# A two-layer decoder trunk: the first two weight tiles in halves, and the last 256 tokens as twice 128

## The chip, the cores and the metric

The kernel runs on one core of a Trainium2 chip. The metric is the time of one execution on the device in microseconds (us), lower is better. Three runs of the kernel before took 2276.80, 2274.09 and 2271.59 us; their median, 2274.09 us, is the time before.

## What is computed

The reference is a decoder trunk of two layers over 1024 tokens with a model width of 1024, in float32. Cut to what matters here:

```python
for l in range(2):
    h = rms_norm(x, norm1[l])
    z = h @ w_in[l]                       # pool | gate u, v | q, k, v
    mix = concat(pool_mixer(...), spatial_gate(...), stick_breaking_attention(q, k, v))
    x = x + mix @ w_out[l]
    h = rms_norm(x, norm2[l])
    x = x + relu(h @ w_up[l])**2 @ w_down[l]   # inner width 4096
return rms_norm(x, final_norm)
```

## The kernel before

**Layout.** Activations lie transposed: 128 features on the partitions, tokens along the free dimension, so x is 8 feature tiles k by 2 chunks c of 512 tokens (chunk 1 holds the first half, as tokens run in reverse). Every matrix product takes its operands as a rounded part and the rest ("hi" and "lo"): `split` (L155 on ScalarE, L156 on VectorE) makes the two, and `mm3` (L235 to L250) adds three products per tile: hi by hi (L243), lo by hi (L248 or L249, by which operand is meant) and hi by lo. A weight tile is 128 rows by 1024 columns; `load_w` fetches it by one DMA of 512 KB into `raw` (L231) and splits it into `wh` and `wl`.

**What sets the order.** The Python code states the work; a tile scheduler then orders the instructions of each engine by its own model of their times, with raised priority for some (`early(W_EARLY)` for the splits of weights, `early(EVAC_EARLY)` for adds that free a PSUM bank). Each engine runs its own list in order. A change of one early instruction can therefore move instructions elsewhere in the lists.

**The start of layer 0.** `load_x` (L477) fetches x tile by tile, all on SyncE's queue: x tile 0, the first weight tile (key columns of the first head pair), x tiles 1 to 3, the second weight tile (query columns), x tiles 4 to 7, then the other chunk. `use_x` scales each x tile by the norm's gain and splits it (`put_x`: ScalarE L166 for hi, VectorE L168 for lo), and sums the squares (`add_sq`: GpSimd L185, ScalarE L183, sums L187 on VectorE and GpSimd). The two weight tiles meet chunk 1 in the loop over k into two PSUM banks (`pkq`, named z), and chunk 0 into two banks named pj. `rms` makes the norm of the tokens: sums by a product with ones (L198, 2 columns each), VectorE L200, a power on GpSimd (L204), a broadcast over partitions by products with the identity (L214), a copy `rbc` (ScalarE L216). With it the two banks are scaled on VectorE (L372 for k, L381 for q), split to `kx`, `qh`, `ql` (L375, L376, L384, L392), and the attention scores begin (L419, L420, L422, into banks z again).

**The MLP.** Up and down projections run as a seven-product scheme on blocks; inner blocks go to DRAM and are read back as `hr` (L946) and split into tiles such as lB (L156). In the down projection the results of PE's banks (po, pg, pj) are added to the residual tiles `acc` (VectorE, L1110), which `load_acc` fetched (L939).

**The end of layer 1.** The last four of the inner feature tiles of the down projection are done plainly, in pieces of tokens given by `TAIL`, as (chunk, first token, tokens). For each piece and each of 8 output tiles m: 12 matmuls into one of 4 po banks, an add into acc on VectorE (L1204), a square on ScalarE (L1206), a sum of squares on GpSimd (L1210). After the eighth, `finish` makes the norm (L198, L200, L204, L214, L216), scales 8 tiles (five on VectorE, L1098; three on GpSimd, L1095 and L1096, by `OUT_POOL`) and sends them by output DMAs (L1100), each of 512 columns in all, in turns from SyncE and ScalarE:

```python
TAIL = ((1, 0, 512), (0, 0, 256), (0, 256, 256))
...
for c, t, n in TAIL:
    for m in range(KT):
        ps = pso()[:, 0:n]
```

Of the kernel before, what the change touches and what calls it, by code (L numbers as in the profile page):

```python
# [7 lines left out]
F32 = mybir.dt.float32  # L8
F32R = mybir.dt.float32r
# [5 lines left out]
P = 128  # L15
S = 1024
D = 1024
KT = D // P
CH = 512
# [16 lines left out]
W_EARLY = 400  # L36
EVAC_EARLY = 400

TAIL = ((1, 0, 512), (0, 0, 256), (0, 256, 256))
OUT_POOL = (2, 5, 6)  # L40
EPS = 1e-6
WINDOWS = ((2, 4), (8, 16))
# [38 lines left out]
def trunk_kernel(tc, xT, w_in, w_out, w_up, w_down, pool_w, sgw, sgb, sgn, cst, outT):  # L81
# [6 lines left out]
    nc = tc.nc  # L88

    with ExitStack() as ctx:  # L90
        per = ctx.enter_context(tc.tile_pool(name="per", bufs=1))
# [27 lines left out]
        def nm(s):  # L119
            uid[0] += 1  # L120
            return f"{s}_{uid[0]}"

        def t512(tag, bufs, dt=F32, pool=None):
            return (pool or per).tile([P, CH], dt, tag=tag, name=nm(tag), bufs=bufs)
# [15 lines left out]
        def early(n):  # L140
            return tc.high_priority(offset=n)
# [4 lines left out]
        def queue(eng, op):  # L146
            if queues[0] is not None:
                if eng in queues[0]:
                    tc.add_manual_dep(
                        op.ins, queues[0][eng], mybir.DependencyInfo(NOSYNC, mybir.DependencyReason.DATA), reason="queue"  # L150
                    )
                queues[0][eng] = op.ins.name

        def split(hi, lo, src):
            queue("act", nc.scalar.copy(hi, src))  # L155
            queue("dve", nc.vector.tensor_sub(lo, src, hi.bitcast(F32)))  # L156
# [68 lines left out]
        def load_w(src, pool=None, tag="w", bufs=2):  # L225

            raw = per.tile([P, D], F32, tag="raw", name=nm("raw"), bufs=2)
            pool = pool or per
            h = pool.tile([P, D], F32R, tag=tag + "h", name=nm(tag + "h"), bufs=bufs)
            lo = pool.tile([P, D], F32R, tag=tag + "l", name=nm(tag + "l"), bufs=bufs)  # L230
            nc.sync.dma_start(raw, src)  # L231
            with early(W_EARLY):
                split(h, lo, raw)
            return h, lo
# [68 lines left out]
        order = []  # L303
# [4 lines left out]
        ready = []  # L308

        def prefetch():  # L310

            if order and order[0] is not None:
                ready.append(load_w(order.pop(0)))
# [13 lines left out]
        for l in range(DEPTH):  # L327
# [8 lines left out]
            with (  # L336
# [137 lines left out]
                def load_x(c, ks):  # L474
                    for k in ks:
                        xs[k, c] = t512(*(("a", NA) if len(xs) % 12 < 8 else ("s", NS)), F32, at)
                        nc.sync.dma_start(xs[k, c], xres[0, k, c])  # L477

                def use_x(c):
                    for k in range(KT):  # L480
                        put_x(k, c, xs[k, c], C_N1)
                    for k in range(KT):
                        add_sq(k, c, xs[k, c], at)

                if l == 0:
                    load_x(1, range(1))
                    prefetch()
                    load_x(1, range(1, 4))
                    prefetch()
                    load_x(1, range(4, 8))  # L490
                    use_x(1)
                    load_x(0, range(8))
                wkq = next_two()
# [164 lines left out]
            with tc.tile_pool(name=f"mx{l}", bufs=1, reuse_waits="tile") as mx:  # L658
# [74 lines left out]
                for c in (1, 0):  # L733
                    t = big()
                    ss = mx.tile([P, 4], F32, tag="ss", name=nm("ss"), bufs=2)
                    for hf in range(2):
                        x = xg[c, hf]
# [10 lines left out]
                    for hf in range(2):  # L748
                        x = xg[c, hf]
# [354 lines left out]
            with tc.tile_pool(name=f"md{l}", bufs=1, reuse_waits="tile") as md:  # L1104
# [15 lines left out]
                for g in range(n_groups):  # L1120
                    bs, b_next = b_next, [{}, {}]
                    for u in range(2):
# [39 lines left out]
                        if g == groups - 1:  # L1162
# [4 lines left out]
                            for m in range(4 * u, 4 * u + 4):  # L1167
                                for c in (1, 0):
                                    x = acc_[m, c]
# [4 lines left out]
                if l == DEPTH - 1:  # L1174
# [3 lines left out]
                    for f in range(4):  # L1178
# [3 lines left out]
                        raw = per.tile([P, D], F32, tag="raw", name=nm("raw"), bufs=2)  # L1182
# [7 lines left out]
                        wd.append(halves)  # L1190
                    for c, t, n in TAIL:
                        for m in range(KT):
# [10 lines left out]
                            x = acc_[m, c][:, t : t + n]  # L1203
# [80 lines left out]
```

## Time and profile before

| | |
|---|---|
| median of three runs | 2274.09 us |
| the profiled execution | 2273.57 us |
| its span, first to last instruction | 2271.7 us |
| mean granted TensorE clock | 0.976 of full speed |
| busy share of the span: PE, VectorE, GpSimd, ScalarE | 94%, 81%, 47%, 42% |

The profile names engines PE (TensorE), PEld (its weight loads), DVE (VectorE), ACT (ScalarE), POOL (GpSimd) and SP (SyncE). The sum of the prediction is made against the profiled execution: 1.87 us of its time lie outside the span. A row of the timeline gives the start, the duration, the engine, the line of the kernel, the operation, the tiles written and read, and in brackets the idle time before it with what ended that.

### The profile page before, as it was taken

The numbers are of one execution on the slowest core, as the hardware profiler recorded it, in microseconds if no ns is written. First come the engines' busy times: TensorE is split into PE (matmuls) and PEld (weight loads), VectorE is DVE, ScalarE is ACT, GpSimd is POOL, SyncE is SP. The second block draws the span as 40 slices with busy tenths as digits, with TensorE's granted clock in tenths as the row PEclk, the third lists the DMA queues.
The fourth block names the chain that finished last, engine by engine and source line by source line (L and its number), as shares of the span: only waits on it lengthen the run. The fifth ranks groups of instructions, "written<-read, shape, count | busy, mean of one in ns | idle before, by whom it ended". The sixth has DMA issues, their size and how long they took to land. (4 is left out here: it accounts for less than half of the span.)

```text
span 2271.7 us, 30343 instructions
## 1 busy us (share of the span) xinstructions
PE 2144.4 (94%) x10608; PEld 1787.6 (79%) x10608; DVE 1830.7 (81%) x2308; ACT 952.0 (42%) x1669; POOL 1070.8 (47%) x851
## 2 busy tenths in 40 slices
PE   7999999979999969999999999997999998999997
PEld 6888897757777758888888888875777776788886
DVE  8788779977777779888868878799677777989864
ACT  5556553443333333333356656435333333333321
POOL 6455556674444433333255646468544444233315
PEclk9999999989999979999999999999999999999998
DMA  3000102235555675554311010133355556755512
GB/s 131 28 29 29 44 25 94 91 117 187 174 176 173 216 261 185 161 192 152 98 52 38 20 47 26 43 93 125 132 182 174 176 174 227 257 190 176 176 43 74
DMA packets 153737, 283.19 MB, mean 125 GB/s; under 512 B 15088, under 2 KB 48368, under 8 KB 153584
## 3 DMA queue, kind: packets, MB, share of 16 engines
q1 hardware_dynamic: 151920, 279.15, 37.2%
q10 hardware_dynamic: 1664, 2.10, 0.3%
q8 instruction: 84, 1.38, 0.2%
q14 instruction: 69, 0.57, 0.1%
HBM read 190.49 MB, written 90.70 MB: 124 GB/s over the span
## 5 line engine op out<-in xcount | busy, mean ns | idle before, releaser
L1000 POOL TENSOR_TENSOR ct<-ct 128x512 f32<-128x512 f32 x128 | 173.8, 1358 | 353.8 <-DVE ct L997 237.3
L434 POOL TENSOR_TENSOR a<-a,s 128x255 f32<-128x255 f32 (+1 forms) x192 | 240.4, 1260 | 181.1 <-ACT a L427 97.0
L836 POOL TENSOR_TENSOR tmp<-rt,raw 128x512 f32<-128x512 f32 x30 | 48.6, 1618 | 344.0 <-DMA rt<-in_w_down 332.1
L243 PE MATMUL pj<-hB,wh 128*128 128x512 f32 x504 | 198.8, 395 | 0.0
L249 PE MATMUL pj<-hB,wl 128*128 128x512 f32 x504 | 197.7, 392 | 0.0
L248 PE MATMUL pj<-lB,wh 128*128 128x512 f32 x504 | 197.7, 392 | 0.0
L1110 DVE TENSOR_TENSOR acc<-acc,po 128x512 f32<-128x512 f32 x240 | 160.6, 679 | 27.4 <-PE po L249 25.3
L991 ACT COPY ct<-po 128x512 f32<-128x512 f32 x66 | 38.8, 588 | 267.0 <-PE po L249 260.5
L155 ACT CAST hT<-hr 128x512 fp32r<-128x512 f32 x122 | 74.9, 620 | 168.4 <-DMA hr<-hd_T 117.4
L458 DVE TENSOR_TENSOR tl<-t,th 128x512 fp32r<-128x512 f32 (+1 forms) x160 | 98.8, 628 | 45.9 <-ACT th L456 44.8
L1012 DVE TENSOR_TENSOR ct<-ct,ct 128x512 f32<-128x512 f32 x120 | 81.3, 699 | 63.0 <-POOL ct L1000 62.0
L431 DVE TENSOR_TENSOR_SCAN s<-s 128x256 f32<-128x256 f32 (+3 forms) x128 | 123.7, 979 | 6.2 <-ACT s L426 5.9
L243 PE MATMUL po<-hB,wh 128*128 128x512 f32 x248 | 99.3, 400 | 26.0 <-ACT wh L155 26.0
L243 PE MATMUL po<-hT,vh 128*128 128x512 f32 x248 | 103.0, 415 | 17.5 <-DVE ct L1054 16.2
L156 DVE TENSOR_TENSOR wl<-rt,wh 128x1024 fp32r<-128x1024 f32 x62 | 110.6, 1784 | 7.1 <-ACT wh L155 7.0
L426 ACT ACTIVATE s<-z 128x256 f32<-128x256 f32 (+1 forms) x192 | 95.4, 500 | 42.9 <-PE z L420 12.3
L243 PE MATMUL po<-hT,wh 128*128 128x512 f32 x256 | 103.1, 403 | 9.8 <-DVE acc L1110 9.7
L243 PEld LDWEIGHTS pj<-hB,wh 128*128 128x128 f32 x504 | 95.3, 189 | 19.7
L248 PEld LDWEIGHTS pj<-lB,wh 128*128 128x128 f32 x504 | 95.3, 189 | 19.7
L249 PEld LDWEIGHTS pj<-hB,wl 128*128 128x128 f32 x504 | 94.9, 188 | 19.9
L156 DVE TENSOR_TENSOR lT<-hr,hT 128x512 fp32r<-128x512 f32 x122 | 97.7, 806 | 14.7 <-ACT hT L155 14.6
L156 DVE TENSOR_TENSOR ct<-ct,ct 128x512 fp32r<-128x512 f32 x64 | 57.2, 893 | 60.0 <-ACT ct L155 60.0
(278 smaller groups left out, 7171.0 us busy)
## 6 DMA issues: line engine op xcount, KB each, us to landing
hd_T<-ct SPq DMA_DIRECT2D x120, 256.0 KB, 2.0
hr<-hd_T SPq DMA_DIRECT2D x120, 256.0 KB, 3.2
raw<-in_w_in SPq DMA_DIRECT2D x36, 512.0 KB, 3.6
raw<-in_w_down SPq DMA_DIRECT2D x34, 512.0 KB, 4.0
raw<-in_w_up SPq DMA_DIRECT2D x32, 512.0 KB, 4.1
rt<-in_w_up SPq DMA_DIRECT2D x32, 512.0 KB, 3.6
rt<-in_w_down SPq DMA_DIRECT2D x30, 512.0 KB, 4.7
hd_B<-ct SPq DMA_DIRECT2D x34, 256.0 KB, 2.0
```

Of the source, the lines that this page charges most:

```text
L155: queue("act", nc.scalar.copy(hi, src))
L156: queue("dve", nc.vector.tensor_sub(lo, src, hi.bitcast(F32)))
L243: mm = nc.tensor.matmul(ps, ah, bh, start=first and i == 0, stop=False, skip_group_check=more)
L248: nc.tensor.matmul(ps, ah, bl, start=False, stop=False, skip_group_check=more)
L249: mm = nc.tensor.matmul(ps, al, bh, start=False, stop=last and i == n - 1, skip_group_check=more)
L426: nc.scalar.activation(s[:, lo:CH], z[:, 0:w], AF.Sigmoid, scale=-ISQ)
L431: nc.vector.tensor_tensor_scan(sl, sl, sl, 1.0 if prev is None else prev[:, CH - 1 : CH], ALU.mult, ALU.bypass)
L434: nc.gpsimd.tensor_mul(a[:, lo + 1 : CH], a[:, lo + 1 : CH], s[:, lo : CH - 1])
L458: nc.vector.tensor_sub(tl[:, 0:wd], pt[:, 0:wd], th[:, 0:wd].bitcast(F32))
L1000: queue("pool", nc.gpsimd.tensor_mul(t, t, t))
L1012: queue("dve", op(t, hb[x], hb[y]))
L1110: (nc.vector.tensor_add if sign > 0 else nc.vector.tensor_sub)(x, x, ps)
```

## The change

Two edits. `TAIL` cuts the last piece of 256 tokens into two of 128. At the start of layer 0 the first two weight tiles are allocated by hand, and fetched and split by halves of 512 columns (k 0 to 3, then k 4 to 7): x tile 0, first half of both weight tiles, x tiles 1 to 3, x tile 4, second half of both, x tiles 5 to 7. Lines from 497 on stand 11 later in the changed kernel (L939 becomes L950, L946 L957, L1110 L1121).

```diff
--- before.py
+++ after.py
@@ -36,7 +36,7 @@
 W_EARLY = 400
 EVAC_EARLY = 400
 
-TAIL = ((1, 0, 512), (0, 0, 256), (0, 256, 256))
+TAIL = ((1, 0, 512), (0, 0, 256), (0, 256, 128), (0, 384, 128))
 OUT_POOL = (2, 5, 6)
 EPS = 1e-6
 WINDOWS = ((2, 4), (8, 16))
@@ -483,11 +483,22 @@
                         add_sq(k, c, xs[k, c], at)
 
                 if l == 0:
-                    load_x(1, range(1))
-                    prefetch()
-                    load_x(1, range(1, 4))
-                    prefetch()
-                    load_x(1, range(4, 8))
+
+                    first_w = []
+                    for _ in range(2):
+                        src = order.pop(0)
+                        raw = per.tile([P, D], F32, tag="raw", name=nm("raw"), bufs=2)
+                        two = [per.tile([P, D], F32R, tag="w" + x, name=nm("w" + x), bufs=2) for x in "hl"]
+                        first_w.append((src, raw, two))
+                        ready.append(tuple(two))
+                    for e in range(2):
+                        half = slice(e * CH, (e + 1) * CH)
+                        load_x(1, range(4 * e, 4 * e + 1))
+                        for src, raw, two in first_w:
+                            nc.sync.dma_start(raw[:, half], src[:, half])
+                            with early(W_EARLY):
+                                split(two[0][:, half], two[1][:, half], raw[:, half])
+                        load_x(1, range(4 * e + 1, 4 * e + 4))
                     use_x(1)
                     load_x(0, range(8))
                 wkq = next_two()
```

The scheduler moves instructions at three places that matter below. First VectorE's list at its start (wl: the lo part of a weight tile; lB: the lo part of an x tile of chunk 1; th: a sum of squares). Before:

```order
L168 SCALAR_TENSOR_TENSOR lB11_16_318<-a_1_288,cs_80,hB11_15_316 128x512
L156 TENSOR_TENSOR wl_4_292<-raw_2_290,wh_3_291 128x1024
L168 SCALAR_TENSOR_TENSOR lB21_18_322<-a_5_296,cs_80,hB21_17_320 128x512
L168 SCALAR_TENSOR_TENSOR lB11_20_326<-a_6_298,cs_80,hB11_19_324 128x512
L168 SCALAR_TENSOR_TENSOR lB21_22_330<-a_7_300,cs_80,hB21_21_328 128x512
L187 TENSOR_TENSOR th_32_350<-th_32_350,tmp_34_355 128x512
L156 TENSOR_TENSOR wl_10_304<-raw_8_302,wh_9_303 128x1024
L168 SCALAR_TENSOR_TENSOR lB11_24_334<-a_11_308,cs_80,hB11_23_332 128x512
L168 SCALAR_TENSOR_TENSOR lB21_26_338<-a_12_310,cs_80,hB21_25_336 128x512
```

With the change:

```order
L168 SCALAR_TENSOR_TENSOR lB11_16_324<-a_7_294,cs_80,hB11_15_322 128x512
L156 TENSOR_TENSOR wl_3_290<-raw_1_288,wh_2_289 128x512
L156 TENSOR_TENSOR wl_6_293<-raw_4_291,wh_5_292 128x512
L168 SCALAR_TENSOR_TENSOR lB21_18_328<-a_8_302,cs_80,hB21_17_326 128x512
L168 SCALAR_TENSOR_TENSOR lB11_20_332<-a_9_304,cs_80,hB11_19_330 128x512
L168 SCALAR_TENSOR_TENSOR lB21_22_336<-a_10_306,cs_80,hB21_21_334 128x512
L187 TENSOR_TENSOR th_32_356<-th_32_356,tmp_34_361 128x512
L168 SCALAR_TENSOR_TENSOR lB11_24_340<-a_11_308,cs_80,hB11_23_338 128x512
L156 TENSOR_TENSOR wl_3_290<-raw_1_288,wh_2_289 128x512
L156 TENSOR_TENSOR wl_6_293<-raw_4_291,wh_5_292 128x512
```

One full split ahead of the second x tile has become two half splits, the first of each weight tile; the second halves come after the fifth x tile, where the second tile's full split stood.

Second, VectorE's list where the start ends: lT and lB are the lo parts of the last x tiles of chunk 0, and L200 begins the norm of chunk 1. Before:

```order
L168 SCALAR_TENSOR_TENSOR lT1_66_481<-a_45_382,cs_80,hT1_65_479 128x512
L168 SCALAR_TENSOR_TENSOR lB22_68_485<-a_46_384,cs_80,hB22_67_483 128x512
L187 TENSOR_TENSOR th_70_489<-th_70_489,tmp_76_506 128x512
L200 TENSOR_SCALAR rst_50_445<-t_49_436 128x4
L156 TENSOR_TENSOR wl_101_605<-raw_99_603,wh_100_604 128x1024
L372 TENSOR_TENSOR tmp_81_528<-z_47_386,rbc_52_453 128x512
```

With the change:

```order
L168 SCALAR_TENSOR_TENSOR lT1_66_487<-a_45_388,cs_80,hT1_65_485 128x512
L200 TENSOR_SCALAR rst_50_451<-t_49_442 128x4
L168 SCALAR_TENSOR_TENSOR lB22_68_491<-a_46_390,cs_80,hB22_67_489 128x512
L187 TENSOR_TENSOR th_70_495<-th_70_495,tmp_76_512 128x512
L156 TENSOR_TENSOR wl_101_611<-raw_99_609,wh_100_610 128x1024
L372 TENSOR_TENSOR tmp_81_534<-z_47_392,rbc_52_459 128x512
```

L200 stands two rows earlier, ahead of the last lB and the last sum of squares.

Third, VectorE's list where layer 0's down projection begins (lT, lB: lo parts of blocks read back, each after its `hr`; acc: residual tiles). Before:

```order
L156 TENSOR_TENSOR lT3_1675_8182<-hr_1676_8183,hT3_1674_8181 128x512
L1110 TENSOR_TENSOR acc_1458_7172<-acc_1458_7172,po_1597_7867 128x512
L156 TENSOR_TENSOR ul_1630_7998<-tmp_1628_7994,uh_1629_7997 128x512
L1110 TENSOR_TENSOR acc_1456_7168<-acc_1456_7168,pg_1599_7869 128x512
L156 TENSOR_TENSOR lB22_1678_8202<-hr_1679_8203,hB22_1677_8201 128x512
L156 TENSOR_TENSOR lB22_1681_8208<-hr_1682_8209,hB22_1680_8207 128x512
L1110 TENSOR_TENSOR acc_1594_7861<-acc_1594_7861,pg_1602_7872 128x512
L1110 TENSOR_TENSOR acc_1594_7861<-acc_1594_7861,po_1600_7870 128x512
```

With the change (both lists end with the second add into acc_1594):

```order
L156 TENSOR_TENSOR lT3_1672_8182<-hr_1673_8183,hT3_1671_8181 128x512
L1121 TENSOR_TENSOR acc_1458_7178<-acc_1458_7178,po_1597_7873 128x512
L156 TENSOR_TENSOR ul_1630_8004<-tmp_1628_8000,uh_1629_8003 128x512
L156 TENSOR_TENSOR lT3_1675_8188<-hr_1676_8189,hT3_1674_8187 128x512
L1121 TENSOR_TENSOR acc_1456_7174<-acc_1456_7174,pg_1599_7875 128x512
L156 TENSOR_TENSOR lB22_1678_8208<-hr_1679_8209,hB22_1677_8207 128x512
L1121 TENSOR_TENSOR acc_1594_7867<-acc_1594_7867,pg_1602_7878 128x512
L1121 TENSOR_TENSOR acc_1594_7867<-acc_1594_7867,po_1600_7876 128x512
```

One lT has moved behind the split of ul, and lB22_1681 has left this place: it comes 8 rows later, among the next group's blocks. On SyncE's list its load, hr_1682, likewise moved from ahead of the eleven acc loads to behind them. On PE's list the first reader of lB22_1681 stands 190 rows behind the first product into pg_1602, in both kernels.

## Rows read from the trace of the kernel before

**Rows 1.** The page of the profile: the span and the engines' busy time.
```profile
span 2271.7 us, 30343 instructions
PE 2144.4 (94%) x10608; PEld 1787.6 (79%) x10608; DVE 1830.7 (81%) x2308; ACT 952.0 (42%) x1669; POOL 1070.8 (47%) x851
```
**Rows 2.** Timeline of DVE at the start: start, duration, engine, line, operation, out<-in, [idle before].
```profile
7.02 1.23 DVE L156 TENSOR_TENSOR wl<-raw,wh 128x1024 fp32r<-128x1024 f32 x1 [0.86 <-ACT wh L155]
```
**Rows 3.** The same timeline of DVE, where the start of layer 0 ends.
```profile
33.50 0.74 DVE L168 SCALAR_TENSOR_TENSOR lB<-a,cs,hB 128x512 fp32r<-128x512 f32 x1
34.17 0.68 DVE L187 TENSOR_TENSOR th<-th,tmp 128x512 f32<-128x512 f32 x1
34.77 0.15 DVE L200 TENSOR_SCALAR rst<-t 128x4 f32<-128x4 f32 x1
35.95 1.23 DVE L156 TENSOR_TENSOR wl<-raw,wh 128x1024 fp32r<-128x1024 f32 x1 [1.03 <-ACT wh L155]
38.54 0.69 DVE L372 TENSOR_TENSOR tmp<-z,rbc 128x512 f32<-128x512 f32 x1 [1.37 <-ACT rbc L216]
```
**Rows 4.** Timeline of PE in the same stretch.
```profile
36.76 1.05 PE L214 MATMUL t<-ident,rst 128*128 128x128 f32 x8
...
38.02 0.36 PE L198 MATMUL t<-ones,tl 128*128 128x2 f32 x2
38.24 0.36 PE L198 MATMUL t<-ones,th 128*128 128x2 f32 x2
...
43.52 0.28 PE L420 MATMUL z<-kx,ql 128*128 128x256 f32 x1
```
**Rows 5.** Timeline of DVE where the down projection of layer 0 begins.
```profile
835.39 3.25 DVE L156 TENSOR_TENSOR lB<-hr,hB 128x512 fp32r<-128x512 f32 x2 [0.75 <-ACT hB L155]
838.56 0.67 DVE L1110 TENSOR_TENSOR acc<-acc,pg 128x512 f32<-128x512 f32 x1
```
**Rows 6.** Timeline of SP's queue there.
```profile
831.50 6.81 SPq L939 DMA_DIRECT2D acc<-xm  x11
```
**Rows 7.** Timeline of PE there.
```profile
839.29 0.80 PE L243 MATMUL pg<-hB,vh 128*128 128x512 f32 x1 [6.90 <-DVE acc L1110]
```
**Rows 8.** Timeline of PE: passes of 128 columns among the attention scores.
```profile
45.04 0.28 PE L419 MATMUL z<-kx,qh 128*128 128x128 f32 x1
45.15 0.28 PE L420 MATMUL z<-kx,ql 128*128 128x128 f32 x1
```
**Rows 9.** Timeline of PE in the last piece of 256 tokens, and behind it.
```profile
2242.93 0.58 PE L243 MATMUL po<-hT,hT 128*128 128x256 f32 x1 [2.64 <-DVE acc L1204]
2243.30 0.42 PE L248 MATMUL po<-lT,hT 128*128 128x256 f32 x1
2243.52 0.42 PE L249 MATMUL po<-hT,lT 128*128 128x256 f32 x1
...
2246.33 0.28 PE L248 MATMUL po<-lB,hT 128*128 128x256 f32 x1
2246.45 0.28 PE L249 MATMUL po<-hB,lT 128*128 128x256 f32 x1
...
2255.42 0.28 PE L249 MATMUL po<-hB,lT 128*128 128x256 f32 x1
2259.71 0.58 PE L198 MATMUL pg<-ones,lT 128*128 128x2 f32 x2 [4.01 <-POOL lT L1210]
...
2261.01 0.57 PE L198 MATMUL pg<-ones,lB 128*128 128x2 f32 x2
2262.61 1.22 PE L214 MATMUL pg<-ident,rst 128*128 128x128 f32 x4 [1.04 <-POOL rst L204]
```
**Rows 10.** Timeline of DVE at the end: the last add and the last five outputs.
```profile
2259.00 0.41 DVE L1204 TENSOR_TENSOR acc<-po,acc 128x256 f32<-128x256 f32 x1
...
2264.28 1.91 DVE L1098 SCALAR_TENSOR_TENSOR hT<-acc,cs,rbc 128x256 f32<-128x256 f32 x2 [2.51 <-ACT rbc L216]
2266.11 1.73 DVE L1098 SCALAR_TENSOR_TENSOR hB<-acc,cs,rbc 128x256 f32<-128x256 f32 x3
```

## The prediction

> **What bounds the kernel now.** I read the page first. PE is busy for 94% of the span and DVE for 81% [rows 1], so over most of the time only PE's own work counts, and neither edit takes matmuls away there. What the change can move lies where PE waits, and I looked for those places in the timelines: the start of layer 0, one long wait at the start of its down projection, and the end. In the start DVE works almost without a pause until it has run L200 at 34.77 [rows 3]; the one pause early on is 0.86 us ahead of the first weight split [rows 2]. In the middle PE stands still for 6.90 us until DVE has done an add [rows 7]. At the end, PE starts its last matmul at 2255.42 [rows 9], DVE's last output ends at 2266.11 + 1.73 = 2267.84 [rows 10], and the span ends at 2271.7 [rows 1], 3.86 us later, by which time the last output transfer has landed. All sums are made against the profiled execution, 2273.57 us, which is 0.5 us under the median of 2274.09.
>
> **Part 1, the weight halves.** Three things happen on DVE's list. First, the split of a half weight waits for 256 KB in place of 512 KB. If the half lands early enough, the pause of 0.86 us goes; it may also stay, as the second tile's half is now wanted early too. I take it as gone. Second, a full split takes 1.23 us [rows 2]; a half split is an operation on 128x512, for which I take 0.68 us, as the sum of the same size takes [rows 3]. Two halves are 1.36, so each tile costs 0.13 more, together 0.26. Third, L200 is moved ahead of an lB (0.74) and a sum (0.68), which together hold it up by 34.77 - 33.50 = 1.27 us [rows 3]. So L200 starts about 0.86 - 0.26 + 1.27 = 1.9 us earlier.
>
> What follows L200 does not keep all of it. The rest of the chain is the power on POOL, the broadcast L214 on PE at 36.76 [rows 4], the copy rbc and L372 at 38.54 [rows 3]. On PE four more products now stand ahead of L214, and the last product of bank pj for k needs the lB that L200 has overtaken; that lB itself ends only about 0.5 us earlier than before (0.86 - 0.26 gained, 0.15 lost to L200). It ended at 34.24 [rows 3], so now at about 33.8; from there some five products of 0.23 us, the spacing of 512 columns, put L214 at about 34.9, 1.8 us earlier than it was. DVE's next weight split, at 35.95 [rows 3], waits for ACT's cast, which waits for that same bank; it moves by 0.5 at most and ends at about 36.7. So L372 can begin at about 36.9, 1.6 us earlier. From L372 a chain on DVE and ACT leads to ql and to L420 at 43.52 [rows 4]; PE, which had products of bank pj up to that point, has run more of them by then, so the scores begin 1.6 us earlier too, and every later stage waits only for work of this chip that moves with it. **Term: -1.6 us, between -3 (the pause, L200's move and earlier starts of PE all kept) and +0.5 (halves do not land earlier, and only their 0.26 and smaller transfers are left).** SP issues two more transfers; its queue is idle for long stretches after the start, and x tiles 5 to 7 come later by those two issues only.
>
> **Part 2, the order in the middle.** This was not intended by the edit, but it is in the lists. PE's wait of 6.90 us ends with the add at 838.56 [rows 5, 7]. Ahead of that add DVE runs two splits lB, 3.25 us together [rows 5], so 1.6 each; one of them now comes later. The add waits as well for acc_1594, whose load is the first of eleven issued from 831.50 on [rows 6]; it is now issued ahead of hr_1682 and so a little earlier. If it has landed by about 837.0, the add moves from 838.56 to 837.0. The lB that was moved out has its reader 190 rows on in PE's list, over 40 us at 0.23 each, which covers its later load. **Term: -1.6 us, between -4 (the wait is cut by both splits' worth) and +2 (a load lands late, or the moved lB holds up adds of the next group).**
>
> **Part 3, the tail.** The matmuls of the last piece double in number, 96 to 192, with half the columns each. Whether this costs anything hangs on what a pass of 128 columns takes. Between attention scores two passes of 128 columns start 0.11 us apart [rows 8]; a pass of 256 columns in the tail takes 2246.45 - 2246.33 = 0.12 [rows 9]; and products of two columns only take 0.22 per pair, 0.11 each [rows 4]. So below 256 columns the length does not show, and what each pass needs beside its columns, the load of its 128x128 weights, sets the spacing. I take 0.11: 96 extra passes are 96 x 0.11 = 10.6 us. The norm of the added piece puts 4 passes L198 and 2 of L214 between them, 0.7 us; the first 128 tokens' passes gain 0.4 over 70 of them at 0.005. So PE's last matmul starts about 11.0 us later, at 2266.4.
>
> Against that stands a shorter chain behind it. Before, it took 2267.84 - 2255.42 = 12.4 us [rows 9, 10]. 3.3 us of it is the last add's wait until 2259.00, while DVE is still scaling the outputs of the piece before; that work now falls beside the matmuls of the last 128 tokens, and the wait goes. From the add to the first output it is 5.28 us [rows 10]; four L198 passes fewer (of eight, 0.43 per pair [rows 9]) save 0.85, two broadcasts fewer of four in 1.22 [rows 9] 0.6, and the narrower add, square and copy 0.3, which leaves 3.5. Five outputs took 1.91 + 1.73, overlapping by a little, 3.56 us [rows 10]; at half the columns I take 1.9, since each has a fixed part. With 0.4 from the last matmul's start to the add that is 5.8 us. DVE's last output then ends at 2266.4 + 5.8 = 2272.2 in place of 2267.84. The last transfers carry 512 columns as before, so the 3.86 us behind them stay. **Term: +4.4 us, between +2 (outputs at 0.3 each, the clock at its upper level for L198 and L214) and +7 (outputs collide with POOL's, last transfers of 128-token rows slower).**
>
> **Sum:** 2273.57 - 1.6 - 1.6 + 4.4 = **2274.8 us**, no change that could be told: 0.2% is 4.5 us, about what a measurement of this kernel can tell from no change.
>
> **Rivals.**
> *Thin passes are cheap* (faster). If a pass of 128 columns streams at 0.06, half of the 0.12, the added 96 cost 5.8 and the first 70 give back 4.2; with 0.7 for the norm PE ends 2.3 later, the chain is 6.6 shorter, and the tail gives -4 if the previous piece's outputs do not hold up the last add, about -1 if they do. With parts 1 and 2 that is 2266.4 to 2269.4. Against it: no row of passes under 256 columns is closer than 0.11 in a run of them. The Trainium skill (TensorE: Matmul & The Clock Gate, section "Back-to-back issue gap") states about 81 ns per pass for a sustained stream of weight loads and matmuls at 128 columns, where the row here shows 110. By that figure I estimate the tail at about -0.6 and the time at 2269.8. Chance 0.15, with a head or middle gain larger than counted in it.
>
> *The clock falls under thin passes* (slower). After PE's wait of 2.64 us passes of 256 columns came 0.22 apart, at the lower clock level, for 3 us [rows 9]. If the granted clock goes down again while PE runs 128 columns at a time, as it did after an idle stretch, passes cost 0.21 to 0.22. It decides from the moment that the fall covers more than about 45 passes: half of the 96 added passes at that level are 48 x 0.11 = 5.3 us more, 2279.5; all 192 are some 18 more, 2292. For it: behind PE's idle 4.01 us the clock was low too [rows 9]. Against it: before the fall PE stood idle each time, and here it does not. Chance 0.1.
>
> *The early gains do not arrive* (nearly slower). The halves land no earlier than the whole did, or a later wait for a load takes up what the head and the middle gave. Then 2273.57 + 4.4 = 2278.0, and with a tail of +7, 2280.6. That a shift of 1 to 2 us early on vanishes behind something fixed speaks against it: PE waits for engines, not for a clock on the wall, at nearly all places I saw. Chance 0.2. That the change does not do what it says (the scheduler's list, not the code, decides when a half is split) is part of it, but DVE's list shows the half splits where they should be.
>
> **How the numbers follow.** The forecast gets 0.55, with 2270 to 2279 as its own range; the three rivals 0.15, 0.1 and 0.2. Faster by over 0.2% is under 2269.5: the cheap passes (0.15) and 0.07 from the forecast's lower edge. Slower is above 2278.6: the clock (0.1), just under half of the third (0.09) and 0.06 of the forecast's upper edge. The range from 2268 to 2281 leaves out the worst of the clock and the best of the cheap passes.
>
> **What would show it.** In the start: no pause ahead of the first half split, L372 near 36.9, the first L420 near 41.9. In the middle: one lB ahead of the add that ends PE's wait, and a wait of some 5 us. In the tail: passes of 128 columns 0.11 apart, PE's last matmul 11 us later counted from the first product after the 2.64 us wait, and no wait of the last add for outputs. I would be wrong if the spacing is clearly under 0.1, if the granted clock falls after that wait, or if a new wait of several us stands in layer 0.

## The result and the profile after

The changed kernel takes 2295.79 us (median of five runs, 2294.48 to 2296.94), the kernel before 2274.09 us beside it. The ratio is 1.0094, with a 95% interval from 1.0079 to 1.0108: **21.7 us slower**, where 2274.8 was forecast in a range from 2268 to 2281. The profiled execution is the run of 2295.79. Its page begins:

```profile
span 2294.1 us, 30595 instructions
PE 2175.8 (95%) x10704; PEld 1818.8 (79%) x10704; DVE 1835.6 (80%) x2324; ACT 953.9 (42%) x1680; POOL 1070.7 (47%) x864
```

Against [rows 1] PE is busy for 31.4 us more with only 96 matmuls more, a third of a microsecond each, and the span grew by 22.4. So I looked where those 31 us lie. DVE's timeline at the start:

```profile
9.06 1.55 DVE L168 SCALAR_TENSOR_TENSOR lB<-a,cs,hB 128x512 fp32r<-128x512 f32 x1 [1.54 <-ACT hB L166]
...
33.48 0.15 DVE L200 TENSOR_SCALAR rst<-t 128x4 f32<-128x4 f32 x1
...
39.59 0.69 DVE L372 TENSOR_TENSOR tmp<-z,rbc 128x512 f32<-128x512 f32 x1 [0.20 <-ACT rbc L216]
```

L200 is 1.3 us earlier than in [rows 3], but L372 is 1.05 later. The early pause did not go, it moved: both half tiles are split at once, and then DVE waits 1.54 us for the second x tile, which now stands behind two transfers. PE's and ACT's timelines show what held up the rest:

```profile
22.13 0.63 PE L249 MATMUL z<-hB,wl 128*128 128x512 f32 x1
22.56 0.63 PE L248 MATMUL z<-lB,wh 128*128 128x512 f32 x1
...
37.82 1.05 PE L214 MATMUL t<-ident,rst 128*128 128x128 f32 x8
...
43.76 0.39 PE L420 MATMUL z<-kx,ql 128*128 128x256 f32 x1
```

```profile
37.09 1.05 ACT L155 CAST wh<-raw 128x1024 fp32r<-128x1024 f32 x1 [9.15 <-PE pj L248]
```

Products of 512 columns come 0.43 apart, the lower clock level. PE then ran without a gap up to the broadcast L214, 1.06 later than in [rows 4], and the cast of the next weight waited for PE. The scores lose less of it: L420 begins 0.24 later than in [rows 4]. In the middle the order did what its rows said; DVE's timeline, then PE's:

```profile
835.75 1.19 DVE L156 TENSOR_TENSOR lB<-hr,hB 128x512 fp32r<-128x512 f32 x1
836.86 0.67 DVE L1121 TENSOR_TENSOR acc<-acc,pg 128x512 f32<-128x512 f32 x1
```

```profile
837.59 0.79 PE L243 MATMUL pg<-hB,vh 128*128 128x512 f32 x1 [5.11 <-DVE acc L1121]
```

One lB stands ahead of the add, PE waits 5.11 in place of 6.90, and the add is done 1.70 us earlier than in [rows 5]. When the tail begins, the change is 0.5 us ahead. The rest is the tail; PE's timeline there:

```profile
2239.29 0.28 PE L248 MATMUL po<-lB,hT 128*128 128x128 f32 x1
2239.40 0.27 PE L249 MATMUL po<-hB,lT 128*128 128x128 f32 x1
2242.44 0.47 PE L243 MATMUL po<-hT,hT 128*128 128x128 f32 x1 [2.77 <-DVE acc L1215]
2242.72 0.41 PE L248 MATMUL po<-lT,hT 128*128 128x128 f32 x1
...
2284.32 0.41 PE L248 MATMUL po<-lB,hT 128*128 128x128 f32 x1
2284.53 0.41 PE L249 MATMUL po<-hB,lT 128*128 128x128 f32 x1
```

The wait is the one of [rows 9], 2.77 for 2.64. It stands behind the first 12 of the 192 thin products (those of 128 columns), which come 0.11 apart. Behind it the other 180 come 0.21 apart, and they still do 42 us later. The table by stretches (start and end, length, the busy time and count of PE, PEld, DVE, ACT and POOL, the granted clock, DMA's share and GB/s) shows why, first of the kernel before, then of the change:

```profile
2242.00:2250.00 8.00, 7.08 (x50) 7.08 (x50) 3.13 (x8) 2.21 (x6) 3.99 (x7) 0.79 0.26 98
2250.00:2256.00 6.00, 5.70 (x50) 5.50 (x48) 2.23 (x6) 1.91 (x5) 4.50 (x7) 1.00 0.00 0
```

```profile
2242.00:2250.00 8.00, 7.56 (x36) 7.56 (x36) 1.83 (x7) 1.58 (x5) 3.26 (x6) 0.50 0.26 98
2250.00:2260.00 10.00, 10.00 (x49) 10.00 (x48) 1.23 (x5) 1.24 (x4) 2.80 (x6) 0.50 0.01 2
2260.00:2285.00 25.00, 25.00 (x119) 25.00 (x119) 8.45 (x21) 3.21 (x11) 9.63 (x19) 0.50 0.20 63
```

Before, the clock was down for a part of the first stretch and full in the second. In the change it is 0.50, the lower level of 1.2 GHz, until PE's last product, although PE does not stop once behind the wait. The last outputs on DVE:

```profile
2284.98 0.29 DVE L1215 TENSOR_TENSOR acc<-po,acc 128x128 f32<-128x128 f32 x1 [2.10 <-PE po L249]
...
2289.76 0.60 DVE L1109 SCALAR_TENSOR_TENSOR hB<-acc,cs,rbc 128x128 f32<-128x128 f32 x2
```

Counted from PE's first product behind the wait: to its last product 42.09 us, before 12.49 [rows 9], so 29.60 longer; from there to the end of DVE's last output 5.83, before 12.42 [rows 9, 10], so 6.59 shorter. With the 0.49 by which the stretch began earlier, and 0.12 at the very end, that is the 22.4 us of the span.

### The profile page after: what moved, and what is told of

It is laid out like the page before. It is cut to its first block, busy times and chain, and to the rows that moved or that the text cites. A ratio compares the mean times of both kernels' runs of the same rounds, so it can differ in the third digit from the quotient of the medians.

```text
span 2294.1 us, 30595 instructions
## 1 busy us (share of the span) xinstructions
PE 2175.8 (95%) x10704; PEld 1818.8 (79%) x10704; DVE 1835.6 (80%) x2324; ACT 953.9 (42%) x1680; POOL 1070.7 (47%) x864
## 5 line engine op out<-in xcount | busy, mean ns | idle before, releaser
L1121 DVE TENSOR_TENSOR acc<-acc,po 128x512 f32<-128x512 f32 x240 | 161.1, 680 | 26.6 <-PE po L249 23.8
L840 POOL TENSOR_TENSOR s<-raw 128x512 f32<-128x512 f32 x62 | 91.4, 1474 | 38.6 <-DVE wl L156 38.6
```

The costliest lines, as they stand in the source:

```text
L840: queue("pool", nc.gpsimd.tensor_add(s1, r["a2"][:, 0], r["a2"][:, 1]))
L1121: (nc.vector.tensor_add if sign > 0 else nc.vector.tensor_sub)(x, x, ps)
```

## The experiments

**Which edit.** Each alone; *head_only* is the change with the old TAIL, *tail_only* the kernel before with the new one:

```diff
-TAIL = ((1, 0, 512), (0, 0, 256), (0, 256, 256))
+TAIL = ((1, 0, 512), (0, 0, 256), (0, 256, 128), (0, 384, 128))
```

> Only the weight halves of the start, TAIL as before. In the trace of the whole change the stages ran 0.5 us earlier than before when the tail began, and the tail was 22.9 us longer from there. Theory (the whole loss is the clock in the tail): about 2273.5 us, between 2270 and 2277, and a granted clock as before behind PE's wait in the tail. Rival (the start and the order it brings cost several us that the trace hides): over 2279.

Measured 2273.74, ratio 0.9986 (0.9976 to 0.9997): the start alone is some 3 us faster, as far as that can be told. Its trace, of the slowest of its twelve executions (2278.35), has the same wait in the tail, 2.64 us until 2247.13, and behind it the clock falls and comes back as before:

```profile
2247.00:2250.00 3.00, 2.87 (x13) 2.87 (x14) 1.07 (x4) 1.07 (x3) 2.74 (x5) 0.50 0.68 257
2250.00:2256.00 6.00, 6.00 (x55) 6.00 (x54) 1.86 (x5) 1.56 (x4) 2.02 (x5) 1.00 0.00 0
```

> Only TAIL changed, the start as before. Theory: the tail alone costs 22.9 us: about 2297, between 2293 and 2300, with 128-column products 0.21 us apart from PE's wait in the tail to the end. Rival (the loss needs both edits): under 2290.

Measured 2298.95 (2297.05 to 2302.32), ratio 1.0098 (1.0085 to 1.0111): the whole loss, 22 us, is the tail's. Its table by stretches:

```profile
2250.00:2286.00 36.00, 36.00 (x170) 36.00 (x170) 9.66 (x24) 4.45 (x15) 12.46 (x25) 0.50 0.14 44
```

**Clock or count.** *wide128* keeps every instruction of the new tail and makes the thin products longer:

```diff
-                            ps = pso()[:, 0:n]
+                            w0 = max(n, 256)
+                            t0 = min(t, CH - w0)
+                            full = pso()[:, 0:w0]
+                            ps = full[:, t - t0 : t - t0 + n]
...
-                                ps,
+                                full,
...
-                                    (tuple(w[:, ms] for w in wd[f][i]), tuple(h[:, t : t + n] for h in hs[f][c]))
+                                    (tuple(w[:, ms] for w in wd[f][i]), tuple(h[:, t0 : t0 + w0] for h in hs[f][c]))
```

> TAIL as in the change, the start as before, but each product of the two pieces of 128 tokens runs over 256 columns, of which 128 are used and the others are thrown away: the same number of products, weight loads, adds, norms and outputs, only longer products. Theory (128-column products let the granted clock stay at its lower level after PE's wait, 256-column products bring it back): the clock is back some 3.4 us after the wait, as before, products come 0.115 to 0.12 apart, and the time falls although more is computed: 11.5 later by 96 more products, 6.6 saved behind the last product, about 2279, between 2276 and 2283. Rival (twice the products, weight loads or small operations of other engines hold the tail at 0.21 per product): 2293 or more, with 0.21 at any length.

Measured 2280.61 (2278.18 to 2289.63), ratio 1.0023 (1.0012 to 1.0035): computing twice the columns takes 17 us off the new tail by the ratios, 18 by the medians. PE's timeline, and the table by stretches:

```profile
2248.70 0.39 PE L243 MATMUL po<-hT,hT 128*128 128x256 f32 x1 [2.64 <-DVE acc L1207]
2248.92 0.28 PE L248 MATMUL po<-lT,hT 128*128 128x256 f32 x1
2249.04 0.28 PE L249 MATMUL po<-hT,lT 128*128 128x256 f32 x1
```

```profile
2250.00:2270.00 20.00, 20.00 (x174) 20.00 (x174) 8.07 (x21) 4.68 (x16) 11.56 (x23) 1.00 0.19 66
```

The same wait, and products 0.12 apart. In this execution the clock did not even fall behind the wait, so its return is not seen here, only in the traces of the kernel before and of head_only. That the number of products, weight loads and small operations costs 0.21 each is ruled out.

**Is the wait needed?** *t384_128* was meant to take it away:

```diff
-TAIL = ((1, 0, 512), (0, 0, 256), (0, 256, 256))
+TAIL = ((1, 0, 512), (0, 0, 384), (0, 384, 128))
...
-                        dst.rearrange("(k p) t -> p k t", p=P), o.rearrange("p (k t) -> p k t", k=per_dma)
+                        dst.rearrange("(k p) t -> p k t", p=P), o[:, 0 : per_dma * n].rearrange("p (k t) -> p k t", k=per_dma)
```

> The start as before, the last 512 tokens as 384 and 128 (outputs of the 384 piece go by single tiles). Four banks of 384 columns are 8.2 us of products, more than the 7 us in which DVE writes the 512-token piece's outputs, so PE should not wait ahead of the thin piece. Theory (the pause starts the fall, thin products only keep the clock from coming back): the 96 products of 128 columns come 0.11 apart; 4.1 saved (pause and slow products behind it), 4.6 lost by longer and shorter products, 6.6 saved at the end: about 2267.5, between 2264 and 2271. Rival (128-column products by themselves let the clock fall): they come 0.21 apart after a while, up to 10 us more, 2272 to 2278.

Measured 2280.02, ratio 1.0015 (1.0006 to 1.0025), 12.5 us over my figure. PE's timeline:

```profile
2246.37 0.33 PE L243 MATMUL po<-hT,hT 128*128 128x128 f32 x1 [0.95 <-DVE acc L1204]
...
2248.87 0.28 PE L248 MATMUL po<-lB,hT 128*128 128x128 f32 x1
2248.99 0.29 PE L249 MATMUL po<-hB,lT 128*128 128x128 f32 x1
2249.10 0.39 PE L243 MATMUL po<-hT,hT 128*128 128x128 f32 x1
2249.29 0.42 PE L248 MATMUL po<-lT,hT 128*128 128x128 f32 x1
```

A wait of 0.95 us was left. Behind it 24 thin products ran 0.11 apart; then, without another wait, the clock fell and stayed low to PE's last product, 19 us later. That does not tell the wait from the thin products. *late_thin* comes nearer: it stands on *late_out*, which writes the outputs of earlier pieces one by one behind later adds (below), so PE never waits ahead of its products, and has the pieces of the change. The other engines' work in the tail lies elsewhere in it too, so the wait is not all that differs.

> late_out with the pieces of the change (512, 256, 128, 128): no wait of PE ahead of the 128-column products. Theory A (128-column products let the granted clock fall by themselves, as 23 of them in t384_128 ran 0.11 apart and the rest 0.21): the fall comes within some 5 us of thin products without a wait, nearly all 192 cost 0.21: 2267.5 + 10.6 + 0.7 - 2.5 + about 16, 2292, between 2287 and 2296. Theory B (a wait of PE is needed, 0.95 us was enough in t384_128): 0.11 to the end: about 2276, between 2273 and 2279.

Measured 2282.36, ratio 1.0036 (1.0015 to 1.0057). In the profiled execution the clock is full through all 192 thin products:

```profile
2243.00:2254.00 11.00, 11.00 (x101) 11.00 (x100) 3.89 (x11) 2.67 (x9) 6.27 (x10) 1.00 0.19 72
2254.00:2266.00 12.00, 12.00 (x110) 12.00 (x109) 5.81 (x14) 3.04 (x10) 8.68 (x14) 1.00 0.30 111
```

```profile
2272.76 0.80 PE L215 MATMUL pg<-ident,rst 128*128 128x128 f32 x2 [5.36 <-POOL rst L205]
```

It is over theory B's 2276 because of its own late outputs: the last broadcast waits 5.36 us for the power, which stands in POOL's queue behind output operations. Of ten executions seven lie between 2277.8 and 2285.7, three between 2292.6 and 2300.0. So theory B has the better of it in most executions; in the three, at a mean clock of 0.968 or 0.969 against 0.974 to 0.977, the clock seems to have fallen without a wait, but there is no trace of one of them. *wide_first* tries the same from the other side, with the wait and only the first thin piece made wide:

```diff
-                            w0 = max(n, 256)
+                            w0 = n if t == 384 else max(n, 256)
```

> As wide128, but only the first of the two 128-token pieces runs over 256 columns (half of them thrown away); the second has products of 128. PE's wait stands ahead of the first. Theory (the clock comes back in the wide piece; 128-column products hold the upper level once they have it and PE does not wait): 0.11 in the second piece, and a time as wide128, ratio 1.002, between 1.000 and 1.004, with single executions some 8 us longer where the clock falls after all. Rival (thin products always lose the clock): 0.21 in the second piece, ratio 1.006 or more.

Measured 2281.00, ratio 1.0021 (1.0011 to 1.0031), as the theory had it. PE's timeline:

```profile
2244.10 0.38 PE L243 MATMUL po<-hT,hT 128*128 128x256 f32 x1 [2.65 <-DVE acc L1207]
...
2255.29 0.27 PE L248 MATMUL po<-lT,hT 128*128 128x128 f32 x1
...
2266.34 0.27 PE L248 MATMUL po<-lB,hT 128*128 128x128 f32 x1
2266.45 0.27 PE L249 MATMUL po<-hB,lT 128*128 128x128 f32 x1
```

The second piece is as thin as in the change and runs at 0.11 from end to end. In this trace too the clock did not fall behind the wait, so it does not show a wide piece bringing it back; a second piece at the lower level would take 96 x 0.102 = 9.8 us more, and the ten executions, 2277.2 to 2284.7, lie closer together than that. Thin products are not slow in themselves; behind a wait they were.

**Taking the wait away for good.** PE's wait in the tail is for an add, and the add for DVE, which writes the first piece's outputs for 7 us; the kernel before, DVE's timeline:

```profile
2235.52 1.89 DVE L1098 SCALAR_TENSOR_TENSOR hT<-acc,cs,rbc 128x512 f32<-128x512 f32 x1 [1.31 <-ACT rbc L216]
...
2242.46 1.40 DVE L1204 TENSOR_TENSOR acc<-po,acc 128x256 f32<-128x256 f32 x4
```

*all256* makes that block shorter by cutting the first piece in two:

```diff
-TAIL = ((1, 0, 512), (0, 0, 256), (0, 256, 256))
+TAIL = ((1, 0, 256), (1, 256, 256), (0, 0, 256), (0, 256, 256))
```

> The start as before, the tail in four pieces of 256 tokens. The first piece's outputs are now 3 to 4 us on DVE in place of 7, less than the 5.5 us of products in four banks, so PE's wait of 2.64 us and the slow products behind it should go. Theory: the clock stays at its upper level to PE's last product, 4.1 saved, 0.3 lost: about 2270, between 2268 and 2273. Rival (the wait is covered by the end anyway): as before, 2272 to 2277.

Measured 2271.10, ratio 0.9972 (0.9961 to 0.9982), 6 us faster. PE's waits in the tail (engine, line, released by; us in all, times, longest) no longer have the one for an add; the longest that is left lies behind the last product:

```profile
PE pg L198 <- POOL lT L1210: 3.5, 1, 3.5
```

*late_out* takes the wait away without cutting the first piece; `finish` hands back its outputs as jobs, and the loop runs them later, each bound behind an instruction on its queue:

```diff
-                            nc.vector.tensor_add(x, ps, x)
+                            dve = nc.vector.tensor_add(x, ps, x).ins.name
...
+                            if pending and m and (end or m >= HOLD):
+                                pending.pop(0)(dve, pool)
+                            if m == KT - 1:
+                                if end:
+                                    for f in pending + final:
+                                        f(dve, pool)
```

> Start and pieces as before (512, 256, 256), but outputs are written later: those of the first piece one by one behind adds of the next pieces, those of the second piece all behind the last add. Theory: PE's wait of 2.64 us ahead of the last piece goes, the clock does not fall (1.5 more), and the last add no longer waits 3.2 us for DVE; one output too many may stand ahead of the last norm (1 back): about 2267.5, between 2265 and 2270. Rival (the delayed outputs only move the wait to the end): 2271 or more.

Measured 2275.00, ratio 0.9987 (0.9977 to 0.9996): 3 us in place of 8 or 9, the rival. DVE's and POOL's timelines at the end:

```profile
2263.99 0.15 DVE L201 TENSOR_SCALAR rst<-pg 128x2 f32<-128x2 f32 x1
```

```profile
2262.54 2.78 POOL L1099 TENSOR_SCALAR hB<-acc,cs 128x256 f32<-128x256 f32 x5
...
2266.65 0.71 POOL L205 TENSOR_TENSOR rst<-rst,mhalf 128x2 f32<-128x2 f32 x1
```

The last norm's mean is there at 2264.14, the power starts at 2266.65: POOL was writing outputs. I had counted DVE's queue and not POOL's.

**The start once more.** *late_head* is late_out with the weight halves, *all256_head* is all256 with them.

> late_out together with the weight halves of the start. If the two are independent it gives late_out times the ratio of head_only, 0.9986: 3 us less than late_out, about 2264.5, between 2262 and 2269. Rival (the gain of head_only was a matter of where the clock fell in the attention, not of the edit): within 1.5 of late_out.

Measured 2269.51, ratio 0.9960 (0.9948 to 0.9973).

> all256 (ratio 0.9972) with the weight halves of the start (0.9986 alone). If the two add up: 0.9958, between 0.994 and 0.9972; some 2266.5 beside a kernel before at 2276. Rival (the halves' gain is the other order in the middle of layer 0 and is lost when the clock falls longer in the start): 0.997 or more.

Measured 2268.63, ratio 0.9972 (0.9958 to 0.9987), the same as all256 without them. So beside late_out the halves bring more than alone, beside all256 nothing. The table by stretches of the start, from 20 to 26 us, in the traces of the change, of head_only and of late_head, whose code there is the same:

```profile
20.00:26.00 6.00, 5.68 (x13) 3.99 (x14) 6.00 (x8) 3.60 (x6) 2.84 (x3) 0.50 0.46 156
```

```profile
20.00:26.00 6.00, 4.89 (x12) 3.59 (x13) 6.00 (x8) 3.58 (x6) 2.84 (x3) 0.59 0.51 165
```

```profile
20.00:26.00 6.00, 5.54 (x18) 3.93 (x18) 6.00 (x8) 3.60 (x6) 2.84 (x3) 0.72 0.42 139
```

L372 begins at 39.59, 40.36 and 37.99 in them, before at 38.54 [rows 3]. The other three traces with the halves agree: a clock of 0.51 there and 39.55 in all256_head, 0.72 and 37.65 in all256_end2, 1.00 and 37.51 in all256_end. In the eight traces with the old start the clock is 0.95 to 1.00 there. So the halves bring L372 forward by 0.5 to 1.0 us where the clock is up for more of that stretch, and cost one or two where it is low for nearly all of it, and only traces with the halves have it that low. What they are worth is about as large as this scatter.

**Better than both.** *all256_end* takes all256_head and binds the outputs of the last piece but one behind the last norm: VectorE's behind its mean, GpSimd's behind its power. *all256_end2* gives GpSimd one of those outputs in place of three:

```diff
+            mean = nc.vector.tensor_scalar(
...
+            root = nc.gpsimd.tensor_tensor(out=r[:, 0:n], in0=r[:, 0:n], in1=mhalf[:, 0:n], op=ALU.pow)
+            norm_ops[:] = [mean.ins.name, root.ins.name]
...
+                                    for f in final if end else ():
+                                        f(*norm_ops)
...
-                    if k % 8 in OUT_POOL:
+                    if k in (OUT_POOL if dve is None else (5,)):
```

> all256_head, and the outputs of the last piece but one are written behind the last norm (VectorE's behind L200, GpSimd's behind the power) instead of ahead of the last adds. Theory: the last add no longer waits 2.3 us, and some 1 us comes back where ten outputs stand in a row: 1 to 2 us less than all256_head. Rival (GpSimd's six outputs in a row become the end): 1 to 2 us more.

Measured 2267.62, ratio 0.9962 (0.9950 to 0.9975): 1 us under all256_head in the medians, inside both intervals. DVE's timeline, then POOL's:

```profile
2250.62 0.42 DVE L1237 TENSOR_TENSOR acc<-po,acc 128x256 f32<-128x256 f32 x1 [0.99 <-PE po L252]
...
2256.33 2.17 DVE L1115 SCALAR_TENSOR_TENSOR hB<-acc,cs,rbc 128x256 f32<-128x256 f32 x3
```

```profile
2257.34 4.46 POOL L1113 TENSOR_TENSOR hB<-hB,rbc 128x256 f32<-128x256 f32 x6
```

The last add comes at once, but GpSimd writes until 2261.80, 3.3 us behind VectorE.

> As all256_end, with GpSimd writing one of the last piece but one's outputs in place of three, VectorE seven in place of five. In all256_end VectorE was through with its last output at 2258.50, GpSimd only at 2261.80. Theory (GpSimd's six outputs in a row are the end there): two of them are 2.7 us of GpSimd, two more on VectorE 1.2, so both end near 2259: 2 us less than all256_end, ratio about 0.995 to the kernel before. Rival (the last transfers set the end, not the engine that writes last): within 0.5 us of all256_end's 0.9962.

Measured 2264.28 (2263.12 to 2265.39), ratio 0.9948 (0.9931 to 0.9966): **some 12 us faster than the kernel before** and 31 faster than the change. GpSimd's last output ends at 2258.23, now shortly before VectorE's at 2258.91:

```profile
2254.76 3.47 POOL L1113 TENSOR_TENSOR hB<-hB,rbc 128x256 f32<-128x256 f32 x4
```

## Why the prediction was wrong

**The step that failed** is the spacing in part 3: "I take 0.11: 96 extra passes are 96 x 0.11 = 10.6 us." The row it came from is right, and 0.11 was measured again (late_thin, wide_first), but only at the upper clock level. PE's last product was forecast 11.0 us later counted from the wait's end; it came 29.6 later. The 180 products behind the wait ran at 0.21 in place of 0.11; some 14 of them were slow in the kernel before too, so 166 of them are 17 of the 18.6 us between, and the products of the norms at the lower level most of the rest. With the 2.7 us by which parts 1 and 2 brought less in the trace (0.5 in place of 3.2), these 18.6 are, to 0.3, the 21.0 us by which the forecast was off. That is my second rival, the clock, with its place, its price for all 192 products (2292) and the right sign, at a chance of 0.1. My reason against it was wrong: I said that PE stands idle before each fall "and here it does not". It does: the wait of 2.64 us is in [rows 9], in front of these very products, and I had used it to count the slow ones. I had taken the return of the clock three microseconds later as given, and that return happened under 256-column products. (The rival's price for half of the added passes should read 2280.1, 2274.8 + 5.3, and not 2279.5.)

**The other rival of part 3** cited the Trainium skill (TensorE: Matmul & The Clock Gate, section "Back-to-back issue gap"), 81 ns per pass for 128 columns. No trace here agrees: in runs of such products 111 to 112 ns at the upper level in late_thin and wide_first, 213 at the lower.

**The chain behind the last product** was right: 5.8 us forecast, 5.83 measured, where two small misses cancel (3.29 in place of 3.5 from the add to the first output, 2.09 in place of 1.9 for the outputs), and 3.86 us at the end is 3.74.

**Part 1**, -1.6 us, fell as a chain of steps. "I take it as gone": the pause of 0.86 came back as one of 1.54 us one x tile later, since that tile now queues behind two halves. And PE was not free to start L214 at 34.9; it was busy with products up to 37.82, because four more stood ahead and the clock was low for the products before. L372 moved by +1.05 in place of -1.6 in this trace, and the scores by +0.24. By the median, head_only is 3 us faster (0.7 to 5.5 by its interval), which happens to be the sum forecast for parts 1 and 2; the traces of the start don't show it as I worked it out. So that number is luck as far as part 1 goes, and part of the gain stays open.

**Part 2** was right: -1.6 forecast, the add 1.70 us earlier than before. It does not all reach the end: 0.5 us are left when the tail begins, and where the rest went was not followed.

## What to carry to other kernels

A price per product read in one place holds at that place's clock: before making products thinner, look at what stands in front of them, and if PE waits there, price them at the lower level until the end; without a wait, three executions of ten in late_thin still lost 10 us or more. Here the better lever was the wait itself, which was another engine writing outputs in one block longer than the banks could cover. Outputs put behind the last norm are free only as far as each engine's own queue is counted, GpSimd's among them.

## What the runs showed of the hardware

The same tail ran faster with twice the columns computed: 2280.6 us in wide128 against 2298.9 in tail_only. Behind a wait of PE of 2.64 us with 256-column products after it, the granted clock fell in two of four traces, for some three microseconds (the kernel before, head_only), and not in the two others (wide128, wide_first). With 128-column products after the wait it fell in all three traces and stayed low to PE's last product, without a gap between the products: for 42 us behind 2.77 us in the change and in tail_only, and for 19 us in t384_128, where the wait was 0.95 us and 24 products came at the upper level first. The same 128-column products held the upper level, 0.11 us each, from end to end in late_thin and in the second piece of wide_first, where they began with it and PE did not wait right ahead of them; three executions of late_thin, 10 to 18 us over its median, suggest that this is not certain.
